# A chunk's second part ahead of the next unit's first part, in the state-space layer of a two-layer decoder step

## The chip, the cores and the metric

One core of a Trainium2 chip runs the whole kernel as one program. The metric is device time in microseconds (us), the median of the timed runs. Engines are named as the profile names them: PE (matmuls), PEld (its weight loads), DVE, ACT and POOL (elementwise work), SP (issues most of the DMAs). Each works through its own queue in program order.

## The reference, cut to what matters

Two groups of tokens, 512 of a prompt and 8x4 of a sample group, pass through one state-space layer (Mamba-2, chunked) and one windowed attention layer with shared keys and values. Everything here concerns the first layer. Its core, for 32 heads in 4 groups and chunks of 128 tokens:

```
cb = einsum("bctgn,bcsgn->bcgts", Cc, Bc)
m = einsum("bcgts,bgjcts->bcgjts", cb, seg)          # seg = exp of decay differences, lower triangle
y_diag = einsum("bcgjts,bcsgjp->bctgjp", m, X)
chunk_states = einsum("bctgn,bgjct,bctgjp->cbgjpn", Bc, decay_in, X)
s_final, s_in = scan(step, s0, (chunk_decay, chunk_states))   # s = decay * s + chunk_state
y_off = einsum("bctgn,cbgjpn,bgjct->bctgjp", Cc, s_in, exp(a_cs))
y = y_diag + y_off
```

Before it stands an input projection (1024 to 5152 columns, a convolution of width 4 and a silu on part of them), behind it a gate, a norm and an output projection.

## The kernel before, in words

**Filler and units.** The input projection is the filler: a generator that yields after every matmul. One projected tile of 128 columns is 24 matmuls into `pa` (256 tokens) and 24 into `pb` (288 tokens): 8 slices of the contraction, three passes each with a high and a low half of the weights (`whi`, `wlo`). For every tile ACT makes `whi` (L205) and DVE `wlo` (L206) from a loaded `wraw`. A conv tile is then copied out by ACT (L343, L348, L349), multiplied once by ACT (L639 `co`) and three times by DVE (L641 `co`); ACT takes a tanh (L643) and DVE writes the result (L644, L645). A z tile takes a tanh on ACT (L680 `zth`) and one DVE operation (L681 `uz`).

The state-space work is cut into units, per group g: chunk 0, chunk 1, quad 0, chunk 2, chunk 3, quad 1. A chunk is 128 prompt tokens of the group's 8 heads, a quad four sample rows. A unit is a generator too. The loop at L915 starts unit u, runs half a pace of filler matmuls (`PACE` is 57, 62, 64 and 44 for the four groups), lets unit u-1 go on to its next part, runs the other half, and lets unit u-1 go on once more.

**A chunk's first part** loads `m` (L728, 512 KB: decay sums, the same for all partitions) and, for c > 0, `ea` (L754); ACT makes decays of it in place with eight Relu (L730) and one Exp (L732); PE makes `cbp` (two products, L734 and L735) and `xp` (four transposes); ACT copies `btok` (L740); DVE makes `xdt`, `xdd`, `cbm` and the masked `m` (L746 to L749).

**A chunk's second part** is on PE `csp` (L757, the chunk's state), for c > 0 `yo` (L765), and `yd` (L774, eight products that read `m` and `xdt`). They are taken out by DVE: `st` (L762, into which POOL has put the decayed old state, L761), `ea` (L767), `v` (L778); in chunk 0 by ACT (L769, L776). It is all the chunk has left: the loop's second call of a chunk finds nothing.

**A quad's first part** loads four states `s` (L804) and makes `cbp`, `xp` and `yos` (L818) on PE; its second part makes `yds`, `yot` and three products `up` (L859), its third a fourth `up`. DVE adds each `up` to a state (L862), and ACT's queue sends the state out (L863).

**Buffers.** All products of the units share one pool of five PSUM tiles (`pss`, L163); `pa` and `pb` have another of three (`pj`, L160). `m` has two buffers, `xdt` and `xdd` together three (L742, L743), `ea` one, the quads' `s` five.

**What sets the order.** PE's order in this layer is that of the code (`pinned`, L139: matmuls are held in program order). The order on DVE, ACT, POOL and SP is set by a scheduler that works from its own model of the times, so it can change with any edit, and no engine leaves its order when the kernel runs.

Of the kernel before, what the change touches and what calls it, by code (L numbers as in the profile page):

```python
# [127 lines left out]
def tile_yoco_step(  # L128
# [569 lines left out]
    def skip_one():  # L698
        if not skips:
            return  # L700
        g, i = skips.pop(0)
        vi = v_t[g][:, i, :]
        nc.vector.scalar_tensor_tensor(vi, xs_t[g][:, i, :], dsk[:, 4 * g + i:4 * g + i + 1], vi, op0=ALU.mult, op1=ALU.add)
        v_done.add((g, i))
        if i < z_done.get(g, 0):
            gate_mul_a(g, i)
# [192 lines left out]
    def run(n):  # L899
        for _ in range(n):  # L900
            if next(fill, 0) == 0:
                return

    units = [(f, (g, i)) for g in range(4) for f, i in
             ((ssm_chunk, 0), (ssm_chunk, 1), (ssm_quad, 0), (ssm_chunk, 2), (ssm_chunk, 3), (ssm_quad, 1))]
# [8 lines left out]
    live = []  # L914
    for u in range(len(units) + 1):  # L915
        pace = PACE[min(u, len(units) - 1) // 6]
        if u < len(units):
            live.append(units[u][0](*units[u][1]))
            next(live[u])
        skip_one()  # L920
        run(pace // 2)
        if u:
            next(live[u - 1], 0)
            skip_one()
            run(pace - pace // 2)
            next(live[u - 1], 0)
            if u == len(units):
                run(10000)
            if u % 6 == 0:
                skips += [(u // 6 - 1, i) for i in range(4)]  # L930
            skip_one()
        else:
            run(pace - pace // 2)
# [702 lines left out]
    def run(n):  # L1636
        m = min(n, ahead[0]) if n > OCN else 0
        ahead[0] -= m
        for _ in range(n - m):
            if next(fill, 0) == 0:  # L1640
                return

    units = [(f, (h, i)) for h in range(ATH - 1) for f, i in
             ((attend, 0), (sample, 0), (attend, 1), (attend, 2), (sample, 1), (attend, 3))]
# [6 lines left out]
    live = []  # L1651
# [113 lines left out]
```

## Time and profile before

| what | value |
|---|---|
| median of 3 runs | 926.12 us (924.83 to 927.18) |
| the profiled execution | 932.11 us; span on the core 930.2 us |
| state-space stage (units on PE) | about 76 to 345 us of the span |
| PE busy, whole span | 908.9 us, 98% |
| DVE, ACT, POOL busy | 687.5, 489.9 and 163.0 us |
| mean granted TensorE clock | 0.996 |

The stages follow each other: input projection and state-space units (to 345 us), output projection, keys and values, attention. A long PE wait shows as idle time before an instruction, with the name of what released it.

### The profile page before, as it was taken

The page shows a single profiled execution, that of the slowest core. Times are in us where ns is not written, and L with a number is a line of the kernel's source. Part 1 is how long each engine was busy: PE and PEld are TensorE (multiplying, and loading weights), DVE is VectorE, ACT ScalarE, POOL GpSimd, SP SyncE. Part 2 cuts the span into 40 slices and gives each one's busy share as a digit, 9 for nine tenths or more (in the row PEclk, how much of TensorE's full clock was granted, in tenths as well). Part 3 has the DMA queues.
Part 4 walks back from the last instruction along what each step waited for, and adds up shares of the span by engine and source line. Part 5 has one row for each costly group of instructions (what it writes and reads, how often), then busy time and mean ns, then how long its engine had stood idle before and what let it go on. Part 6 is the DMA issues. An engine that isn't in the chain of part 4 may idle for free.

```text
span 930.2 us, 21888 instructions
## 1 busy us (share of the span) xinstructions
PE 908.9 (98%) x8671; PEld 847.9 (91%) x8671; DVE 687.5 (74%) x1435; ACT 489.9 (53%) x1140; POOL 163.0 (18%) x212
## 2 busy tenths in 40 slices
PE   8999999999999999999999999999999999999997
PEld 7989888888989889999999999999899999989997
DVE  6998899989799899644489335876677766778732
ACT  6678655655566655422255213555455555557642
POOL 2031344433514642111101001000000000000021
PEclk9999999999999999999999999999999999999999
DMA  8224365355364442536277556757768868774511
GB/s 295 93 74 155 104 206 166 121 170 170 134 201 161 149 165 101 156 108 228 90 256 227 183 184 196 265 182 264 252 203 262 280 204 267 270 256 155 194 49 49
DMA packets 80573, 168.48 MB, mean 181 GB/s; under 512 B 19990, under 2 KB 37736, under 8 KB 79960
## 3 DMA queue, kind: packets, MB, share of 16 engines
q1 hardware_dynamic: 73784, 154.60, 50.5%
q10 hardware_dynamic: 5616, 9.75, 2.8%
q0 software_dynamic: 1072, 2.74, 1.1%
q8 instruction: 68, 1.11, 0.5%
q14 instruction: 33, 0.27, 0.1%
HBM read 141.14 MB, written 25.93 MB: 180 GB/s over the span
## 4 chain that ended last, share of the span: by engine, by line
PE 82%; DVE 9%; DMA 4%; ACT 2%; issue 2%; POOL 0%; SPq 0%; POOLq 0%; DVEq 0%; ACTq 0%
PE pa L146 33%; PE pb L146 28%; PE sp L146 3%; PE pv L146 2%; PE so L146 2%; PE s L146 2%; DVE wlo L206 2%; DMA kc<-ck 1%; PE yd L146 1%; DMA m<-aed 1%; DVE co L641 1%; PE csp L146 1%; PE w L149 1%; PE ptp L149 1%; PE xp L149 1%
## 5 line engine op out<-in xcount | busy, mean ns | idle before, releaser
L205 ACT ACTIVATE whi<-wraw 128x1024 fp32r<-128x1024 f32 x69 | 72.8, 1056 | 97.0 <-PE pb L146 57.2
L206 DVE TENSOR_TENSOR wlo<-wraw,whi 128x1024 fp32r<-128x1024 f32 x69 | 89.6, 1298 | 45.1 <-ACT whi L205 44.7
L146 PE MATMUL pa<-bq,whi 128*128 128x272 f32 x512 | 103.1, 296 | 0.0
L146 PE MATMUL pb<-nl,whi 128*128 128x288 f32 x280 | 84.0, 300 | 0.0
L146 PE MATMUL pb<-nh,wlo 128*128 128x288 f32 x280 | 83.5, 298 | 0.0
L146 PE MATMUL pb<-nh,whi 128*128 128x288 f32 x280 | 83.4, 298 | 0.0
L146 PEld LDWEIGHTS pa<-bq,whi 128*128 128x128 f32 x512 | 81.2, 189 | 0.9
L146 PE MATMUL pa<-nh,whi 128*128 128x256 f32 x280 | 81.1, 290 | 0.5 <-DVE uz L681 0.5
L146 PE MATMUL pa<-nl,whi 128*128 128x256 f32 x280 | 80.7, 288 | 0.0
L146 PE MATMUL pa<-nh,wlo 128*128 128x256 f32 x280 | 80.1, 286 | 0.0
L146 PE MATMUL pb<-bq,whi 128*128 128x272 f32 x384 | 77.2, 296 | 1.3 <-DVE kv L1230 1.1
L146 PE MATMUL pa<-bq,wlo 128*128 128x272 f32 x256 | 74.2, 290 | 0.0
L641 DVE SCALAR_TENSOR_TENSOR co<-cb,cvp,co 128x568 f32<-128x568 f32 x72 | 64.0, 892 | 1.5 <-ACT co L639 0.9
L146 PEld LDWEIGHTS pb<-bq,whi 128*128 128x128 f32 x384 | 60.8, 189 | 2.6 <-DVE kv L1230 1.3
L1289 ACT ACTIVATE whi<-wraw 128x512 fp32r<-128x512 f32 x64 | 40.1, 627 | 35.2 <-PE pb L146 16.8
L146 PEld LDWEIGHTS pb<-nl,whi 128*128 128x128 f32 x280 | 53.0, 189 | 4.4 <-issue 4.4
L146 PEld LDWEIGHTS pa<-nh,whi 128*128 128x128 f32 x280 | 53.8, 192 | 2.6 <-issue 1.9
L146 PE MATMUL pb<-bq,wlo 128*128 128x272 f32 x192 | 55.5, 289 | 0.0
L146 PEld LDWEIGHTS pa<-nl,whi 128*128 128x128 f32 x280 | 53.8, 192 | 1.4 <-issue 1.4
L146 PEld LDWEIGHTS pb<-nh,wlo 128*128 128x128 f32 x280 | 53.1, 190 | 2.2 <-issue 2.2
L146 PEld LDWEIGHTS pa<-nh,wlo 128*128 128x128 f32 x280 | 53.8, 192 | 0.9 <-issue 0.9
L146 PEld LDWEIGHTS pb<-nh,whi 128*128 128x128 f32 x280 | 53.0, 189 | 0.8 <-issue 0.8
(408 smaller groups left out, 2788.0 us busy)
## 6 DMA issues: line engine op xcount, KB each, us to landing
wraw<-w_in SPq DMA_DIRECT2D x40, 512.0 KB
kc<-ck SPq DMA_DIRECT2D x32, 640.0 KB
vc<-cv SPq DMA_DIRECT2D x32, 640.0 KB
wraw<-wb SPq DMA_DIRECT2D x32, 512.0 KB
s<-s SPq DMA_DIRECT2D x32, 256.0 KB
m<-aed SPq DMA_DIRECT2D x16, 512.0 KB
ssmS<-s ACTq DMA_DIRECT2D x32, 256.0 KB
wraw<-w_out SPq DMA_DIRECT2D x16, 512.0 KB
```

The source lines that it names most:

```text
L146: pin(nc.tensor.matmul(*a, **k))
L149: pin(nc.tensor.transpose(*a))
L205: a = nc.scalar.activation(hi, raw, AF.Copy)
L206: b = lo_eng.tensor_tensor(lo, raw, f32(hi), op=ALU.subtract)
L641: nc.vector.scalar_tensor_tensor(o, cb[:, k:k + n], cvp[:, ti, k:k + 1], o, op0=ALU.mult, op1=ALU.add)
L1289: nc.scalar.activation(hi, src[p][j], AF.Copy)
```

## The change

Where unit u-1 is a chunk, its second part now stands directly ahead of unit u's first part, and the two calls half a pace and a whole pace later are left out. Quads go as before. No instruction is added or taken away.

```diff
     for u in range(len(units) + 1):
         pace = PACE[min(u, len(units) - 1) // 6]
+
+        joined = u and units[u - 1][0] is ssm_chunk
+        if joined:
+            next(live[u - 1], 0)
         if u < len(units):
             live.append(units[u][0](*units[u][1]))
             next(live[u])
         skip_one()
         run(pace // 2)
         if u:
-            next(live[u - 1], 0)
+            if not joined:
+                next(live[u - 1], 0)
             skip_one()
             run(pace - pace // 2)
-            next(live[u - 1], 0)
+            if not joined:
+                next(live[u - 1], 0)
```

Below, chunk c of group g is written g.c. Three places show how the rows move.

On PE, where chunk 0.1 ends and quad 0 of group 0 begins (filler rows left out between the rows shown: 28 in the kernel before). Before:

```order
L149 MATMUL cbp<-ident,bp 128x128
L146 MATMUL cbp<-CT,bp 128x16
L149 MATMUL xp<-ident,xpd 128x128 x4
L146 MATMUL yos<-s_1279,cp 32x512
L146 MATMUL yos<-s_1281,cp 32x512
L146 MATMUL yos<-s_1283,cp 32x512
L146 MATMUL yos<-s_1285,cp 32x512
```

and, 28 filler rows later:

```order
L146 MATMUL csp<-xdd,btok 128x512
L146 MATMUL yo<-CT,st 128x128 x4
L146 MATMUL yd<-m,xdt 64x128 x8
```

Now:

```order
L146 MATMUL csp<-xdd,btok 128x512
L146 MATMUL yo<-CT,st 128x128 x4
L146 MATMUL yd<-m,xdt 64x128 x8
L149 MATMUL cbp<-ident,bp 128x128
L146 MATMUL cbp<-CT,bp 128x16
L149 MATMUL xp<-ident,xpd 128x128 x4
L146 MATMUL yos<-s_1300,cp 32x512
```

The chunk's three PSUM tiles and the quad's three are now asked for in one run of rows: six out of a pool of five. The same holds at both quads of each group.

On DVE, the rows up to the removal of `csp` of chunk 1.1 (`st`). Before:

```order
L681 SCALAR_TENSOR_TENSOR uz<-zth,pa 128x256
L829 TENSOR_TENSOR xdt<-xp,tok 128x512
L644 SCALAR_TENSOR_TENSOR CT<-cb,co 128x512
L645 SCALAR_TENSOR_TENSOR CT<-cb,co 128x32
L220 SCALAR_TENSOR_TENSOR btr<-cbp,csts,btr 128x128
L823 TENSOR_TENSOR cbs<-cbp,csts 128x16
L839 TENSOR_TENSOR ms<-ms,cbs 128x128
L206 TENSOR_TENSOR wlo<-wraw,whi 128x1024
L681 SCALAR_TENSOR_TENSOR uz<-zth,pb 128x288
L832 TENSOR_TENSOR xdd<-xp,tok 128x512
L762 TENSOR_TENSOR st<-csp,st 128x512
```

Now:

```order
L644 SCALAR_TENSOR_TENSOR BT<-cb,co 128x512
L645 SCALAR_TENSOR_TENSOR BT<-cb,co 128x32
L641 SCALAR_TENSOR_TENSOR co<-cb,cvp,co 128x568
L681 SCALAR_TENSOR_TENSOR uz<-zth,pa 128x256
L641 SCALAR_TENSOR_TENSOR co<-cb,cvp,co 128x568
L762 TENSOR_TENSOR st<-csp,st 128x512
L767 TENSOR_TENSOR ea<-yo,ea 128x512
```

`st` has moved up past the quad's rows and one `wlo`; ahead of it stand still the `co` and `uz` rows of filler tiles.

On ACT, the rows ahead of the second quad of group 0, with the evacuation of the filler tile that PE ends there (L348 to L639) and the Relu and Exp of chunk 1.0 (`m`). Before:

```order
L643 ACTIVATE cb<-co 128x568
L205 ACTIVATE whi<-wraw 128x1024
L348 COPY cb<-pb 128x256
L349 COPY cb<-pb 128x8x4
L219 ACTIVATE btr<-cbp,csts 128x128
L635 COPY cvo<-cb 128x27
L639 ACTIVATE co<-cb,cvp 128x568
L825 COPY yos<-yos 128x512
L730 ACTIVATE m<-m,tok 128x128 x6
```

Now:

```order
L730 ACTIVATE m<-m,tok 128x128 x6
L732 ACTIVATE m<-m 128x1024
L205 ACTIVATE whi<-wraw 128x1024
L348 COPY cb<-pb 128x256
L349 COPY cb<-pb 128x8x4
L643 ACTIVATE cb<-co 128x568
L635 COPY cvo<-cb 128x27
L639 ACTIVATE co<-cb,cvp 128x568
L219 ACTIVATE btr<-cbp,csts 128x128
L825 COPY yos<-yos 128x512
```

The Relu and Exp rows have gone from behind the tile's evacuation to ahead of it. With them the load of that `m` has moved in SP's queue: before it stood behind four loads of quad states and a `wraw`, now it stands behind two of the four.

## Prediction

> **What bounds the kernel now.** I read the page's busy times first, then the table by stretches over the state-space stage, with groups 1 and 2 and a short stretch of 2 us, then PE's waits from 60 to 345 us (in all, times, longest).
>
> ```profile
> PE 908.9 (98%) x8671; PEld 847.9 (91%) x8671; DVE 687.5 (74%) x1435; ACT 489.9 (53%) x1140; POOL 163.0 (18%) x212
> ```
> ```profile
> core 0: us, PE busy (x) PEld busy (x) DVE busy (x) ACT busy (x) POOL busy (x), PEclk, DMA share, GB/s
> 140.00:211.00 71.00, 69.32 (x573) 61.78 (x572) 66.82 (x94) 42.80 (x109) 28.50 (x31) 1.00 0.46 153
> 211.00:290.00 79.00, 75.44 (x592) 67.49 (x591) 68.36 (x105) 45.92 (x116) 28.97 (x31) 0.96 0.51 166
> 216.00:218.00 2.00, 2.00 (x12) 2.00 (x11) 2.00 (x4) 1.97 (x6) 0.00 (x0) 0.50 0.29 88
> ```
> ```profile
> PE xp L149 <- DVE xs L644: 2.1, 1, 2.1
> PE up L146 <- DVE cbm L748: 1.4, 1, 1.4
> PE yd L146 <- ACT yos L825: 1.2, 1, 1.2
> PE pa L146 <- DVE uz L681: 0.5, 1, 0.5
> ```
>
> PE bounds the stage, and DVE stands close behind: 66.82 of 71 us in group 1. The waits list says that PE loses 5.2 us. The short stretch shows what a wait costs besides: just behind the 2.1 us wait the granted clock is 0.50. The first rows behind that wait and behind the 1.4 us wait (at 214.63 and 258.83), picked out of the chain of waits, each below the same work undisturbed:
>
> ```profile
> 70.11 2.85 PE pa L146 x24
> 214.63 4.20 PE pa L146 x24
> 239.08 2.32 PE pb L146 x16
> 258.83 3.12 PE pb L146 x16
> ```
>
> The same matmuls took 4.20 instead of 2.85 us after the first wait, 1.35 us more, and after the second the first sixteen alone took 0.8 us more. I take 1.35 for both, 2.7 together. (Group 1, with the waits of 1.2 and 0.5 us, kept a granted clock of 1.00.) So all that a better order could win here is 5.2 + 2.7 = 7.9 us, 0.85% of the kernel.
>
> **The change, part by part.** PE has the same matmuls before and after. What changes is when the others must have delivered.
>
> *Inputs of the second part.* `csp`, `yo` and `yd` come half a pace (28 to 32 filler matmuls, about 0.12 us each by the x24 row, so some 3.5 us) sooner behind the first part. Of the 16 chunks 0.0 had the least time between its masked `m` and `yd`:
>
> ```profile
> 81.43 1.22 DVE L749 TENSOR_TENSOR m<-m,cbm 128x1024 f32<-128x1024 f32 x1
> ```
>
> `m` was done at 82.65 and `yd` ran at 89.95 (row below), 7.3 us later. Cost 0; the cover that is left is some 3.8 us, and where DVE falls that much further behind, `yd` itself waits (-0, +3 at one place). Something is freed too: `xdd` of odd chunks had to wait for the previous chunk's `csp` to give up one of three buffers, and now does not. I give this no price of its own; it shows in the places of the rows below.
>
> *Fewer changes between filler and units.* One return to filler is saved per chunk. The rows from the chain:
>
> ```profile
> 85.06 0.44 PE xp L149 x4
> 85.50 1.07 PE pa L146 x9
> ...
> 89.95 1.02 PE yd L146 x16
> 90.97 0.86 PE pb L146 x5
> ```
>
> Behind `xp` a filler matmul takes 0.12 us, as always; the five behind `yd` take 0.17 instead of 0.13, 0.2 us together. Over 16 chunks the gain is 0 to 3.2 us; I take the middle, -1.6, since no row shows `yd` followed by `cbp`.
>
> *PSUM, the new wait.* Where a quad follows a chunk (twice per group), six tiles in a row are asked of five buffers, so the quad's `yos` must wait until DVE has taken out `csp` (`st`, L762). Behind `yos` the filler is queued, so all of PE stands. The time that PE gives to DVE is what lies between:
>
> ```profile
> 100.25 0.86 PE csp L146 x2
> 101.11 0.89 PE yo L146 x8
> 102.00 1.02 PE yd L146 x16
> ```
>
> ```profile
> 161.48 0.27 PE L149 MATMUL cbp<-ident,bp 128*128 128x128 f32 x1
> 162.30 1.06 PE L146 MATMUL yos<-s,cp 128*32 128x512 f32 x8
> ...
> 167.17 1.02 PE L146 MATMUL csp<-xdd,btok 128*128 128x512 f32 x2
> ```
> ```profile
> 168.65 0.41 DVE L681 SCALAR_TENSOR_TENSOR uz<-zth,pa 128x256 f32<-128x256 f32 x1
> ...
> 175.83 0.68 DVE L762 TENSOR_TENSOR st<-csp,st 128x512 f32<-128x512 f32 x1
> ```
>
> `yo` and `yd` take 0.89 + 1.02, the quad's `cbp` and `xp` 0.82 (161.48 to 162.30): 2.7 us from the end of `csp` to `yos`, 3.6 from its start. Before, `st` ended 8.3 us behind `csp` at 1.1 (168.19 to 176.51), and no matmul stood waiting for it. What stands ahead of `st` now, at each place (`csp` now begins where the quad's `cbp` stood):
>
> - 0.1: two `co` of a tile whose evacuation was long done. No stall.
> - 0.3: ACT has the Relu and Exp of chunk 1.0 ahead of the tile's evacuation, and that needs its `m`. Rows of ACT and SP:
>
> ```profile
> 118.20 5.36 SPq L804 DMA_DIRECT2D s<-s  x4
> 124.13 0.38 SPq L728 DMA_DIRECT2D m<-aed  x1
> ```
> ```profile
> 128.86 1.04 ACT L205 ACTIVATE whi<-wraw 128x1024 fp32r<-128x1024 f32 x1
> 130.51 0.87 ACT L639 ACTIVATE co<-cb,cvp 128x568 f32<-128x568 f32 x1
> 131.74 1.87 ACT L730 ACTIVATE m<-m,tok 128x128 f32<-128x128 f32 x6
> 134.55 1.06 ACT L732 ACTIVATE m<-m 128x1024 f32<-128x1024 f32 x1
> ```
> ```profile
> 195.97 7.81 DMA m<-aed
> 250.54 4.32 DMA m<-aed
> ```
>
>  The load goes out behind two of the four `s` loads, at about 120.9, and takes 4.3 to 7.8 us: 125.2 at best. Then eight Relu (8/6 x 1.87 = 2.5), Exp 1.06, `whi` 1.04, three copies and a tanh (some 1.4) and `co` 0.87: 132.1; DVE's `co` and `st`, some 0.75 each, with what lies between: 134. PE is at `yos` at 131.5 (the quad's `cbp` stood at 127.9). Stall 0.5 (landing early, rows overlapping) to 5; I take 2.7.
> - 1.1: DVE is the late one. `st` now stands directly behind the `uz` of 168.65 and a `co`, so it ends at 169.7 at the earliest, if DVE, which is full here, has the same work ahead; PE wants `yos` at 161.5 + 3.6 = 165.1. That is 4.6 us; if the stall at 0.3 has already let DVE catch up, 0.5. I take 2.6.
> - 1.3 and 2.1: the first Relu rows of the next chunk but one (2.0, 2.2) have moved ahead of the evacuation on ACT, where they wait for `m`.
>
> ```profile
> ACT m L730 <- DMA m<-aed: 12.9, 8, 3.6
> ```
> ```profile
> 189.12 6.29 SPq L804 DMA_DIRECT2D s<-s  x3
> 195.97 0.38 SPq L728 DMA_DIRECT2D m<-aed  x1
> ```
>
>  For 1.3 the load goes out behind two of the three `s`, at 193.3, lands at 197.6 to 201.1, and the same string on ACT and DVE (some 6.5 us) ends `st` at 204 to 207.6; PE is at `yos` at 202.2. Stall 0 to 5.6, I take 3.0. For 2.1, reckoned in the same way, 0 to 3: 1.6.
> - 2.3, 3.1, 3.3: the rows ahead of `st` are of tiles done a half before, or z tiles with one short DVE operation. 0.3 in all.
>
> Together 10.2 us of new stalls (bounds 1 and 19). A stall of 1.4 us or more has cost 1.35 us more at the low clock: three of four such, 4.1. Behind a stall PE comes later to everything, so DVE, which was the late one at the four old waits, is in time there: the old 5.2 and 2.7 us go.
>
> The Trainium skill, "TensorE: Matmul & The Clock Gate", section "Why this matters for your kernels", says that only idle gaps over about 3 us between bursts bring the clock down. By it neither old nor new stalls would cost clock, and the sum would be 10.2 - 5.2 - 1.6 = 3.4 us. The row at 216 us, behind a gap of 2.1 us, says otherwise, and the trace decides.
>
> *SP and POOL.* Loads of `m` go out up to 5 us sooner, since `yd` of the chunk two back is done sooner; the distance from that `yd` to the use is what it was. POOL's `st` product (L761) needs the previous chunk's state, a whole pace away as before. Cost 0 each; bounds -1 and +1 by a landing that shifts a neighbour.
>
> **The sum.** New stalls 10.2, clock 4.1, old waits -5.2, old clock loss -2.7, changes saved -1.6: +4.8 us. The profiled execution took 932.11 us, so 936.9; it ran 0.65% above the median of 926.12, so I put the difference on the median: 930.9.
>
> **The rivals.**
>
> *The waits only change their place.* In group 1 DVE has 66.82 us of work in 71; PE must wait for it somewhere, now or later. If the stalls at 0.3 and 1.1 let DVE catch up, 1.3 and 2.1 do not stall: 5.6 us of stalls, 2.7 of clock, -9.5 of old: -1.2, 925. For it speaks the full DVE; against it that at 1.3 and 2.1 a DMA is late, which PE's coming later does not help, since the loads move with it. Chance 0.22 for within 0.3%, the least that a measurement here can tell from no change (2.8 us).
>
> *Faster.* `st` is in time everywhere: then nothing is lost, and 7.9 + 1.6 = 9.5 us can go, of which I would expect two thirds: -6.3, 920. This decides where `st` ends within 2.7 us of `csp`. For it: `st` now stands higher in DVE's queue, and `xdd` needs no free buffer. Against: DVE needed 8.3 us at 1.1. Chance 0.20.
>
> *Much slower.* ACT stands on its first Relu until `m` lands, and each of the four stalls is near its upper bound: 18 us, clock 5.4, -9.5 of old: +14, 940. For it: 7.81 us for one load. Chance 0.13; the forecast itself has 0.45.
>
> So slower 0.58, same 0.22, faster 0.20. The range leaves out about one in ten on each side: 919 to 940; the forecast's own is 928 to 936.
>
> **What would show it.** In the profile after: a wait of PE `yos` on DVE `st`, two to four times, 1 to 5 us, at the quads that follow 0.3, 1.1, 1.3 and 2.1; low granted clock behind them; the four old waits gone or smaller; the ACT waits on `m` not below 12.9 us. If PE shows no `yos` wait, the forecast is wrong in its main term; if the old waits are still there beside the new, it is too low.

## The result, and the profile after

The changed kernel took 948.74 us in the median of five runs (945.91 to 951.50), the kernel before 927.18 in the same comparison (924.83 to 927.85): a ratio of 1.0241, 95% interval 1.0215 to 1.0267, or 21.6 us. The forecast was slower, 930.9 in a range of 919 to 940: the sign and the place were right, the size was not.

The profiled execution of after took 948.74 us, its median; that of before, 932.11, lay 5 us above its own. In spans they differ by 16.7 us (946.9 and 930.2). Outside the state-space stage before took 1.7 us longer than after (641.8 us in after, 643.5 in before), with late loads as the visible part (PE waited 2.2 us for the first weights at 6 us and 1.4 for `kc`, against 0.5 and nothing), so inside the stage the difference is larger, 18.4 us.

The whole stage in one row each, from its first `cbp` to the first matmul of the projection behind it (columns as in the tables of the prediction: the stretch, its length, busy us of PE, PEld, DVE, ACT and POOL, granted clock, DMA share, GB/s). Before:

```profile
76.70:363.42 286.72, 281.46 (x2293) 251.19 (x2291) 257.88 (x386) 173.74 (x418) 111.31 (x116) 0.99 0.47 155
```

After:

```profile
76.39:381.52 305.13, 285.66 (x2292) 252.90 (x2291) 260.18 (x386) 173.21 (x418) 111.21 (x116) 0.97 0.45 145
```

PE stands 19.5 instead of 5.3 us (length less busy time), and its work takes 4.2 us more at a lower clock. DVE's work is nearly the same, 260 and 258 us, but DVE stands 45 us instead of 29. PE's waits in the stage of after:

```profile
PE yos L146 <- DVE st L762: 17.1, 5, 5.2
PE xp L149 <- DVE xs L644: 2.1, 2, 1.8
PE pa L146 <- DVE uz L681: 0.3, 1, 0.3
```

The wait that the prediction named is there and is nearly all of it: the quad's `yos` on `st`, five times, at 131.3 (behind chunk 0.3, 2.1 us), 168.6 (1.1, 4.5), 210.3 (1.3, 3.0), 251.6 (2.1, 2.4) and 290.1 (2.3, 5.2). The last is the one that the prediction had dismissed. SP, ACT, DVE and PE there, each in order of time:

```profile
280.47 0.42 SPq L728 DMA_DIRECT2D m<-aed  x1
```
```profile
288.62 0.40 ACT L730 ACTIVATE m<-m,tok 128x128 f32<-128x128 f32 x1 [8.89 <-DMA m<-aed]
288.93 1.04 ACT L205 ACTIVATE whi<-wraw 128x1024 fp32r<-128x1024 f32 x1
...
291.19 0.86 ACT L639 ACTIVATE co<-cb,cvp 128x568 f32<-128x568 f32 x1
```
```profile
290.01 1.23 DVE L206 TENSOR_TENSOR wlo<-wraw,whi 128x1024 fp32r<-128x1024 f32 x1 [5.12 <-ACT whi L205]
...
292.08 2.50 DVE L641 SCALAR_TENSOR_TENSOR co<-cb,cvp,co 128x568 f32<-128x568 f32 x3
294.50 0.68 DVE L762 TENSOR_TENSOR st<-csp,st 128x512 f32<-128x512 f32 x1
```
```profile
286.25 1.02 PE L146 MATMUL csp<-xdd,btok 128*128 128x512 f32 x2
...
295.24 1.08 PE L146 MATMUL yos<-s,cp 128*32 128x512 f32 x4 [5.19 <-DVE st L762]
```

Read them from the top. The load of chunk 3.0's `m` goes out at 280.5 and takes 8.1 us. ACT has its first Relu at the head of its queue and stands 8.89 us for it. Behind the Relu stands a weight's high part (`whi`), which does not read `m` at all; DVE's low part (`wlo`) waits for that, 5.12 us; behind it are a conv output and three taps, and only then `st`. `csp` had been done since 287.1, where `yo` begins; `st` takes it out at 294.5, 7.4 us later. The matmuls that stand between take up 2.9 of these; the rest PE waits.

### The profile page after: what moved, and what is told of

The parts are those of the page before. It is cut to its first block, busy times and chain, and to the rows that moved or that the text cites. A ratio compares the mean times of both kernels' runs of the same rounds, so it can differ in the third digit from the quotient of the medians.

```text
span 946.9 us, 21901 instructions
## 1 busy us (share of the span) xinstructions
PE 914.0 (97%) x8671; PEld 851.1 (90%) x8671; DVE 690.0 (73%) x1435; ACT 489.9 (52%) x1140; POOL 162.9 (17%) x212
## 4 chain that ended last, share of the span: by engine, by line
PE 81%; DVE 8%; DMA 4%; ACT 4%; issue 2%; SPq 0%; POOL 0%; POOLq 0%; DVEq 0%; ACTq 0%
PE pa L146 33%; PE pb L146 27%; DMA m<-aed 3%; PE sp L146 3%; PE pv L146 2%; PE so L146 2%; PE s L146 2%; DVE wlo L206 1%; DVE co L641 1%; PE yos L146 1%; PE w L149 1%; PE ptp L149 1%; PE yd L146 1%; PE csp L146 1%; DVE v L703 1%
## 5 line engine op out<-in xcount | busy, mean ns | idle before, releaser
L641 DVE SCALAR_TENSOR_TENSOR co<-cb,cvp,co 128x568 f32<-128x568 f32 x72 | 62.1, 864 | 1.9 <-ACT co L639 0.9
L730 ACT ACTIVATE m<-m,tok 128x128 f32<-128x128 f32 x128 | 42.1, 393 | 24.7 <-DMA m<-aed 24.7
```

What stands on the lines that cost most here:

```text
L641: nc.vector.scalar_tensor_tensor(o, cb[:, k:k + n], cvp[:, ti, k:k + 1], o, op0=ALU.mult, op1=ALU.add)
L730: nc.scalar.activation(m_t[:, h, :], m_t[:, h, :], AF.Relu, scale=-1.0, bias=tok[:, c, 0, 8 * g + h:8 * g + h + 1])
```

## The experiments

All stand against the kernel before in runs of the same comparison, where its median was 927.1 to 927.6. Theories: **R**, the loss is the run of six tiles in five buffers (the ring); **T**, the second part is due half a pace sooner from engines without slack, and the ring is only the first place where that shows; **L** or **O**, the loads of `m` and the Relu rows on ACT; **2**, R and L side by side; **S** and **Q**, DVE's slack or the order of the queues; **P**, POOL's adds (later). Each edit also lets the scheduler choose a new order on DVE, ACT, POOL and SP, so a difference of a microsecond or two need not come from what the edit is meant to change.

| kernel | median, us | ratio to before, 95% interval |
|---|---|---|
| changed | 948.74 | 1.0241 (1.0215 to 1.0267) |
| `join_cc` | 940.65 | 1.0130 (1.0109 to 1.0151) |
| `join_cq` | 934.04 | 1.0070 (1.0053 to 1.0087) |
| `after_yos24` | 947.97 | 1.0214 (1.0194 to 1.0234) |
| `eighth` | 941.11 | 1.0150 (1.0125 to 1.0176) |
| `quarter` | 930.76 | 1.0042 (1.0028 to 1.0056) |
| `late34` | 923.88 | 0.9963 (0.9950 to 0.9976) |
| `late78` | 926.38 | 0.9979 (0.9967 to 0.9991) |
| `after_mhold` | 941.07 | 1.0159 (1.0137 to 1.0181) |
| `before_nom` / `after_nom` | 927.23 / 936.65 | 1.0001 (0.9990 to 1.0013) / 1.0096 (1.0077 to 1.0115) |
| `yos24_nom` | 934.15 | 1.0062 (1.0042 to 1.0082) |
| `before_tap` / `after_tap` | 923.47 / 935.53 | 0.9957 (0.9942 to 0.9972) / 1.0098 (1.0074 to 1.0123) |
| `before_nom_tap` / `after_nom_tap` | 924.70 / 928.69 | 0.9977 (0.9960 to 0.9993) / 1.0022 (1.0009 to 1.0034) |
| `before_nossq` / `after_nossq` | 922.05 / 941.37 | 0.9946 (0.9928 to 0.9963) / 1.0150 (1.0133 to 1.0168) |
| `after_nom_tap_nossq` | 921.82 | 0.9941 (0.9926 to 0.9956) |

### Half of the change each, and a yos that comes later

`join_cc`, `join_cq`: which joins are kept.

```
-        joined = u and units[u - 1][0] is ssm_chunk
+        joined = u and u < len(units) and units[u - 1][0] is ssm_chunk and units[u][0] is ssm_chunk
```

(`join_cq` with `is not ssm_chunk` at the end.)

> Only the joins from chunk to chunk are kept; where a quad follows, the chunk's second part stands half a pace later, as before. Theory R (ring: the loss is the quad's yos, sixth of six tiles in five PSUM buffers, which waits for DVE's st): no yos wait on st, the old waits somewhere between 0 and 5 us; 920 to 928, same as before or a little faster. Theory T (time: the second part comes half a pace too early for a full DVE and ACT wherever it is joined; the ring is only the first place where that shows): about half of the loss stays, 935 to 940, as waits of csp, yd or xp.

> Only the joins from chunk to quad are kept. Theory R: all of the loss is here, yos waits on st of 14 to 20 us in all, 943 to 952. Theory T: about half of it, 935 to 940.

`after_yos24`: a `yield` ahead of the quad's `yos`, and 24 filler matmuls there.

```
+        late = 24 * (u < len(units) and units[u][0] is ssm_quad)
+        run(late)
+        if late:
+            next(live[u])
-        run(pace // 2)
+        run(pace // 2 - late)
```

> The changed kernel, but the quad's yos matmuls come 24 filler matmuls (2.9 us) behind its xp, so DVE has 5.6 instead of 2.7 us from the end of csp. Theory R: each yos wait is 2.9 us shorter: 2.1, 4.5, 3.0, 2.4, 5.2 become 0, 1.6, 0.1, 0, 2.3, 4 us in all, and most of the low clock goes: 928 to 935. Theory T: DVE and ACT deliver no sooner, so other matmuls wait in its place (yot, up, xp, yd); the sum of PE's waits in the stage stays at 12 us or more, 940 or more.

R fell in all three. PE's longest waits in the stage, of `join_cc`, of `join_cq` and of `after_yos24`:

```profile
PE xp L149 <- DVE xs L644: 6.6, 2, 3.4
PE yd L146 <- ACT yos L825: 1.4, 2, 1.0
```
```profile
PE yos L146 <- DVE st L762: 4.8, 2, 3.8
PE xp L149 <- DVE xs L644: 3.9, 2, 2.5
```
```profile
PE xp L149 <- DVE xs L644: 12.3, 2, 6.3
PE yos L146 <- DVE st L762: 3.2, 4, 1.5
PE up L146 <- DVE cbm L748: 1.8, 1, 1.8
```

`join_cc` has no `yos` wait on `st` and still costs 13 us. In `after_yos24` the `yos` waits shrink as reckoned, from 17.1 to 3.2 us, and nothing is won: PE now stands 12.3 us for `xs` at the start of groups 2 and 3. The buffer ring says where PE waits, not how long. That is T's picture, though T's numbers for the two halves (equal parts) were off too. ACT's wait for `m` went to different sides: 31.8 us in `join_cc` and 5.7 in `join_cq`, against 12.9 before; that this makes the halves unequal was not tested.

### Where the second part stands

`eighth`, `quarter`, `late34`, `late78`: the chunk's second part at 1/8, 1/4, 3/4 and 7/8 of the pace behind the following unit's first part (the changed kernel is 0, the kernel before 1/2), here `quarter`:

```
-        run(pace // 2)
+        run(pace // 4)
+        if u and units[u - 1][0] is ssm_chunk:
+            next(live[u - 1], 0)
+        run(pace // 2 - pace // 4)
```

> The kernel before with a chunk's second part an eighth of a pace (5 to 8 filler matmuls, about 0.8 us) behind the following unit's first part. No yos waits on st, since csp comes behind yos. Theory 2: the run of six tiles now ends with yd, which needs only the quad's cbp to be taken out, so that part goes; the loads of m are drawn forward nearly as far as in the changed kernel, so 932 to 940. Theory T: between the quarter (930.8) and none (948.7), near 940.

> The kernel before with a chunk's second part a quarter of a pace behind the following unit's first part (half a pace in the kernel before, directly ahead in the changed one). The run of six tiles is gone. Theory T: cost in proportion to the time taken away, 934 to 940. Theory O: m is given up a quarter sooner, so also a cost, but jumpy: 927 to 940. If only the run of six tiles mattered: 924 to 928.

> The kernel before with a chunk's second part three quarters of a pace behind the following unit's first part. Theory T: more time for DVE, so 918 to 925. Theory O: m is given up later still, loads and Relu rows stand later; ACT's wait for m below 12.9 us, 920 to 927, unless m's own product then comes late and yd of the chunk after next waits.

> The kernel before with a chunk's second part seven eighths of a pace behind the following unit's first part. At three quarters PE's waits in the stage were down to 0.9 us, so there is little left to win: 921 to 926. If the state or m's buffer now comes late (m is given up an eighth later still), waits of yd or csp: 925 to 930.

In order of the place: 948.7, 941.1, 930.8, 927.1, 923.9, 926.4. The later the second part, the better, up to three quarters; the steep part is the first quarter, which gives back 18.0 of the 21.6 us. `quarter` came out better than T had said (934 to 940) and inside O's range (927 to 940); the cost is not in proportion to the time taken away. For `eighth` theory 2 said 932 to 940 and T near 940, and the time hardly tells them apart. The waits do:

```profile
PE xp L149 <- DVE xs L644: 5.4, 2, 3.2
PE yd L146 <- DVE cbs L823: 4.5, 2, 3.5
ACT m L730 <- DMA m<-aed: 9.4, 6, 3.2
```

ACT stands less for `m` than in the kernel before (12.9 us), so the loads do not explain these 13.5 us; and `yd`, the sixth tile here, now waits until the quad's `cbp` has been taken out (`cbs`), which theory 2 had held to be free. PE waits for DVE in another place, as T has it. The stage of `late34`:

```profile
78.10:357.70 279.60, 277.55 (x2293) 248.01 (x2291) 255.10 (x386) 173.96 (x419) 114.06 (x116) 1.00 0.48 158
PE pa L146 <- DVE uz L681: 1.2, 1, 1.2
PE yos L146 <- ACT st L769: 0.9, 1, 0.9
```

Two waits are all that is left, 2.1 us, the first of them at the stage's very end, and the clock is 1.00. `late34` beats both kernels; it is 0.4% faster than before. At 7/8 (926.4 us, just above the 921 to 926 expected) the wait of this kind has grown again. By the medians that place is too late, but the two intervals overlap:

```profile
PE yos L146 <- ACT st L769: 2.3, 2, 1.2
```

### The loads of m

`after_nom`, `before_nom`: no loads of `m`; the Relu reads a constant tile.

```
-        dma(m_t, dap(aed, (32 * c + 8 * g) * 128, [[0, 128], [128, 8], [1, 128]]))
-            nc.scalar.activation(m_t[:, h, :], m_t[:, h, :], AF.Relu, scale=-1.0,
+            nc.scalar.activation(m_t[:, h, :], tri, AF.Relu, scale=-1.0,
```

> The changed kernel without the 16 loads of m (512 KB each): the Relu reads a constant tile instead, so ACT never stands on a load there; instructions on PE, DVE and ACT are the same in number. Theory L (load: ACT's Relu waits for m, behind it the weight's high part and DVE's low part, behind that st): the yos waits at 0.3, 1.3, 2.1 and 2.3, 12.7 us in all, fall below 1 us each, only 1.1 may keep up to 4.5; 925 to 934. If st is late by DVE's own amount of work and its order (theory D): yos waits of 12 us or more stay, 942 or more.

> The kernel before without the 16 loads of m (the Relu reads a constant tile). It is the partner of the changed kernel without loads, 936.7. Theory O: the cost of the change comes through the loads, so the two should lie within 3 us of each other: 933 to 938 here. Theory T: the change costs without loads too; this one stays at 920 to 928, and the difference to 936.7 is 9 us or more.

Before does not miss the loads (1.0001), as T said; O had put the two kernels within 3 us of each other. After is 12.1 us faster without them, but 9.4 us remain, so L is a part and not the whole, and its own number (925 to 934) was missed. The `yos` waits at 0.3, 1.3 and 2.3 are gone, as L said; 4.6 us at 1.1 remain, and 2.0 at 2.1, where L had put less than 1.

`after_mhold`: one DVE operation of a single element reads `m` behind `v`, so that `m`'s buffer is given up later.

```
+ nc.vector.tensor_tensor(hold[0:1, 0:1], m_t[0:1, 0, 0:1], v[0:1, 0, c * 128:c * 128 + 1], op=ALU.add)
```

> The changed kernel with one more DVE operation of a single element per chunk, which reads m and v behind v: m's buffer is given up some 3 to 6 us later, so the load of m for the chunk after next and its Relu rows stand later on SP and ACT, behind the high part of a weight that was behind them. PE's order is that of the changed kernel. Theory O (order: m given up sooner draws loads and Relu rows forward in queues that work in order, ACT stands on the load, and behind it whi, wlo and the conv chain): ACT's wait for m falls from 24.7 to 13 us or less and DVE's wait for whi from 25.7 to 18 or less; 928 to 938. Theory T (time: outputs of the second part are due half a pace sooner from a DVE with no slack): 943 to 951, the waits only change their place.

It won 7.7 of 21.6 us, between the two theories. DVE's wait for `whi` fell as O had said; the expected fall of ACT's own wait did not come. ACT's wait for `m` in before, after and `after_mhold`, and then DVE's wait for `whi` in the same three:

```profile
ACT m L730 <- DMA m<-aed: 12.9, 8, 3.6
```
```profile
ACT m L730 <- DMA m<-aed: 24.7, 8, 8.9
```
```profile
ACT m L730 <- DMA m<-aed: 24.2, 11, 4.4
```
```profile
DVE wlo L206 <- ACT whi L205: 19.2, 14, 3.1
```
```profile
DVE wlo L206 <- ACT whi L205: 25.7, 11, 5.1
```
```profile
DVE wlo L206 <- ACT whi L205: 6.8, 8, 1.6
```

So it is not the sum of ACT's standing that costs, but what is queued behind it while it stands. At 1.3 and 2.3 the Relu rows now come behind `whi` and the tile's evacuation (at 2.3 `co` runs at 279.2 and the first Relu at 282.3), and the `yos` waits of 3.0 and 5.2 us there are gone. At 0.3 the first Relu still stands ahead of `whi`, and 1.0 us of wait is left.

`yos24_nom` takes away both, the loads and the short time that DVE has until `yos`.

> The changed kernel without the loads of m and with the quad's yos 24 filler matmuls later: both suspected causes are taken away at once. Theory 2 (two causes: loads and Relu rows drawn forward, 12 us; the run of six tiles where DVE is behind, 9.5 us): 925 to 930, PE's waits in the stage below 5 us. Theory T (DVE has half a pace less, and every way of waiting for it costs the same): the yos waits turn into waits of xp, up or pa, 934 to 938.

934.2 us lies in T's range, not in theory 2's. Without loads and with `yos` 2.9 us later PE still waits 4.2 us for `xs`, 1.6 for `st` and 1.5 for `uz`.

### DVE's slack

One of the three convolution taps on DVE (L641) is left out in four kernels: change or not, loads or not. From 76.7 to 363.4 us the taps that stay kept DVE busy for 30.7 instead of 49.8 us in the kernel before and 32.0 instead of 47.9 in the changed one, 16 to 19 us less.

```
-        for k in range(1, 4):
+        for k in range(1, 3):
```

> The kernel before with two instead of three taps of the convolution on DVE (one is left out): 18 operations of 0.92 us, 16.6 us, less for DVE in the stage. PE's waits in the stage of before, 5.2 us with 3 us of low clock, should shrink to 0 to 2 us: 919 to 925.

> The changed kernel with one tap of the convolution left out, so DVE has 16.6 us of slack in the stage. Theory S (no slack: the half pace taken from DVE can't be given by a full engine): with slack the difference to its partner before falls from 21.6 to 5 us or less, 920 to 930. Theory Q (queue order: ACT stands on a load of m and DVE behind it, whatever DVE has to do): the 12 us that hang on the loads stay, 932 to 940.

> The kernel before without loads of m and with one tap left out: the floor for the stage, 918 to 925.

> The changed kernel without loads of m and with one tap left out. Theory S: no more than 3 us over its partner before, no yos wait over 1 us; 919 to 927. If the 9.5 us that the change costs without loads came from order alone (each queue in its new order, whatever the slack), 6 us or more of it stay: 927 to 933.

The cost of the change (after less before, of the medians):

| | with loads of `m` | without |
|---|---|---|
| three taps | 21.6 | 9.4 |
| two taps | 12.1 | 4.0 |

Both matter, and neither alone is the cause. Slack takes away about half in each column; the part that hangs on the loads stays at 8 to 12 us in each row, so Q holds for it. `after_tap` came where Q put it; `after_nom_tap` lies, by its cost of 4.0 us, between the two (its time, 928.7, in the range for order alone). What was left there was in the main one place, 1.1:

```profile
PE yos L146 <- DVE st L762: 5.7, 2, 4.6
```

### What is late at 1.1

The wait at the quad behind 1.1 was much the same in the changed kernel, `after_mhold`, `after_nom`, `after_tap` and `after_nom_tap` (4.5 to 4.8 us), with loads or without, with three taps or two. DVE and POOL of the changed kernel there:

```profile
159.83 0.68 DVE L746 TENSOR_TENSOR xdt<-xp,tok 128x512 f32<-128x512 f32 x1
...
162.67 2.40 DVE L749 TENSOR_TENSOR m<-m,cbm 128x1024 f32<-128x1024 f32 x1
164.98 1.88 DVE L641 SCALAR_TENSOR_TENSOR co<-cb,cvp,co 128x568 f32<-128x568 f32 x1
166.79 2.37 DVE L206 TENSOR_TENSOR wlo<-wraw,whi 128x1024 fp32r<-128x1024 f32 x1
169.08 0.80 DVE L641 SCALAR_TENSOR_TENSOR co<-cb,cvp,co 128x568 f32<-128x568 f32 x1
...
172.27 0.68 DVE L762 TENSOR_TENSOR st<-csp,st 128x512 f32<-128x512 f32 x1
```
```profile
159.29 1.52 POOL L761 TENSOR_TENSOR st<-st,dec 128x512 f32<-128x512 f32 x1
160.78 1.36 POOL L711 TENSOR_TENSOR v<-v,uz 128x544 f32<-128x544 f32 x1
162.10 5.97 POOL L716 TENSOR_TENSOR ssq<-ssq,uz 128x544 f32<-128x544 f32 x3
```

While POOL adds the squares of group 0's gate (L716), DVE's rows take twice their time: `m` 2.40 instead of 1.21 us, a tap 1.88 instead of 0.80, `wlo` 2.37 instead of 1.21. `before_nossq`, `after_nossq`, `after_nom_tap_nossq` leave these adds out:

```
-        nc.gpsimd.tensor_tensor(ssq, ssq, uz, op=ALU.add)
```

> The kernel before with POOL's adds of the squares (ssq, L716, 15 in all) left out; DVE's order stays. DVE rows that stood beside them (m at 156.59: 2.36 instead of 1.22 us) take their usual time. Theory P (POOL's long adds slow DVE beside them, and that is the lateness at 1.1): the old waits at 169 and 175, 1.7 us, go: 923 to 927. Without it: 926 to 929.

> The changed kernel with POOL's adds of the squares left out. Theory P: the four DVE rows between 161.2 and 169.1, which took 8.2 us, take 4.6; the yos wait at 1.1 falls from 4.46 to below 1.5 us, the one at 2.1 by 1 us; 940 to 945. Without it: 946 to 951, and 4 us or more of wait at 1.1.

> The changed kernel without loads of m, with one tap left out and without POOL's adds of the squares. With loads and taps gone, all that was left of PE's waits was yos, 4.64 at 1.1 and 1.06 at 2.1, and 4.0 us against its partner (928.7 to 924.7). Theory P: both waits below 1 us and 923 to 926, nothing of the change's cost is left. Without it: the 4.6 us stay, 927 to 930.

P holds for the place. In `after_nossq` the same DVE rows take their usual time:

```profile
164.47 1.21 DVE L749 TENSOR_TENSOR m<-m,cbm 128x1024 f32<-128x1024 f32 x1
165.60 0.80 DVE L641 SCALAR_TENSOR_TENSOR co<-cb,cvp,co 128x568 f32<-128x568 f32 x1
166.32 1.21 DVE L206 TENSOR_TENSOR wlo<-wraw,whi 128x1024 fp32r<-128x1024 f32 x1
```

The wait at 1.1 fell from 4.5 to 1.0 us and the kernel to 941.4. The wait at 2.1, which should have lost 1 us, did not (2.4 and 2.7). Without loads it was 2.0, with a tap less besides 1.1, and with the adds gone too it was not seen: no single one of the three takes it away. Before gained 5.0 us as well, a little more than expected, so the adds are a tax on both kernels and explain only some 2.3 us of the difference (21.6 less 19.3). With loads, one tap and adds gone, the changed kernel stands at 921.8, under `before_nom_tap` (924.7, which still has the adds), and one `yos` wait of 1.7 us remains, at 1.1, not below 1 as expected. What of the change's cost is left there is not measured, since a kernel before without all three was not run. If the adds cost it the same 5.0 us as above, it would stand near 919.7, and some 2 us would be left; that is an estimate.

## Why the prediction was wrong in size

The table has the prediction's own terms in us, and beside them what the two profiled executions show. The low clock is summed over stretches of 1 us, busy time of PE times what its clock lacked of 1.00. The changes saved are what is left over of PE's busy time (4.2 us more in after, 5.1 of them by the clock), and so were not measured by themselves.

| term | forecast | measured |
|---|---|---|
| `yos` at 0.3 | 2.7 | 2.1 |
| at 1.1 | 2.6 | 4.5 |
| at 1.3 | 3.0 | 3.0 |
| at 2.1 | 1.6 | 2.4 |
| at 2.3, 3.1, 3.3 and 0.1 | 0.3 | 5.2, at 2.3 |
| low clock, new | 4.1 | 8.5 |
| old waits | -5.2 | -2.9 |
| old low clock | -2.7 | -3.4 |
| changes saved | -1.6 | -0.9 |
| sum, in the stage | 4.8 | 18.4 |

- **Place and mechanism: right.** The wait that was named, on the tile that was named, at the four places that were named. At 0.3 the working (load, eight Relu, Exp, `whi`, conv, `st`) came as written and was 0.6 us off. At 1.3 the 3.0 us are partly luck: the load took 7.7 us, the upper end of its range, only one Relu and no Exp stood ahead of `whi`, and PE itself came later to `yos`. Its signs came, too: such waits (five instead of two to four), low clock behind some, ACT's wait for `m` at 24.7 us, above the 12.9 of before. So did its sign of being too low: the `xp` wait on `xs` was still there beside the new ones, 2.1 us in both kernels.
- **The step that failed first: "2.3 ... 0.3 in all".** The wait there was 5.2 us, the largest single miss of the sum. The step looked at the rows that DVE has directly ahead of `st` and took their tiles for long done. It did not follow them to ACT: at 2.3, as at 1.3, the `whi` ahead of them was queued behind the first Relu of the next group's chunk, whose load was 8.1 us on its way. The rule that had been applied at 1.3 was not applied at 2.3; with 1.3's own bounds, 0 to 5.6, it would have held.
- **1.1: the middle instead of the end.** The row gave 4.6 if DVE has the same work ahead; the rival "it has caught up by then" was mixed in at half weight. DVE could not catch up, since POOL's adds were slowing it; without them the wait was 1.0 us. The adds had rows in the trace of before too; there `m` of 1.1 took 2.36 us, and 1.21 without them.
- **"Behind a stall DVE is in time there: the old 5.2 and 2.7 us go."** Wrong by nearly half for the waits: PE still waited 2.1 us for `xs`, the wait that also stood first in `join_cc` and `after_yos24`. A stall of PE does not let DVE catch up when DVE itself stands on ACT through it: DVE's wait for `whi` rose from 19.2 to 25.7 us.
- **The clock: 8.5 instead of 4.1.** Four waits cost clock, three had been counted: the two long ones cost double, 6.8 us at half clock instead of 3.4, two of the `yos` waits (3.0 and 2.4 us) cost none, and one of `xp` (1.85 us) did. The last section has the rows.
- **"SP and POOL ... Cost 0 each."** Right for what was counted, the issue and the state's product; wrong in that the earlier loads drew the Relu rows forward on ACT. The prediction had those rows in its 0.3, 1.3 and 2.1, but not as one cause; without the loads the changed kernel was 12.1 us faster.
- **The rivals.** "Much slower" had 18 us of stalls where 17.1 came, but by luck: its four places gave 12.0 of them, the rest came at 2.3. It still ended at 940: its clock loss was 5.4 where 8.5 came, and it took away 9.5 us of old waits, old clock and savings where 7.2 went.
- The median moved by 21.6 us, the stage of the profiled executions by 18.4. The 3.2 us between them are not traced to a place.

## What to carry to other kernels

Giving a buffer up sooner is no gain by itself: here the scheduler pulled the next load and its first reader forward in queues that work in order, and what stood behind that reader then waited for the DMA. When PE and a second engine are both near full, price a move by the lead that it takes from the second engine and not by the first wait that becomes visible; loosening that wait (24 matmuls more ahead of `yos`) moved it and won next to nothing. Try the opposite direction too: here the second part a quarter of a pace later was the faster kernel.

## What the runs showed of the hardware that was not expected

**The clock falls on a grid.** These rows show the granted clock (the last column but two) in and behind four gaps of PE in after. Of the gap at 1.1, which ended at 173.01, only the low stretch is shown, which began inside it.

```profile
131.32:133.40 2.08, 0.00 (x1) 0.00 (x0) 2.08 (x5) 0.73 (x2) 1.77 (x5) 1.00 0.50 114
133.48:136.88 3.40, 3.40 (x15) 1.74 (x16) 3.40 (x5) 1.21 (x2) 1.51 (x2) 0.50 0.83 309
171.02:177.84 6.82, 4.83 (x21) 3.17 (x22) 6.79 (x14) 4.53 (x11) 4.68 (x9) 0.50 0.41 156
210.29:213.24 2.95, 0.00 (x0) 0.00 (x0) 2.88 (x5) 2.95 (x9) 1.63 (x4) 1.00 0.90 342
213.24:217.00 3.76, 3.76 (x29) 2.92 (x30) 3.65 (x6) 2.81 (x6) 2.63 (x3) 1.00 0.36 124
223.06:224.91 1.85, 0.00 (x1) 0.01 (x1) 1.11 (x3) 1.46 (x2) 0.00 (x0) 1.00 0.38 153
225.64:229.04 3.40, 3.40 (x18) 3.40 (x17) 3.40 (x6) 0.00 (x0) 0.00 (x0) 0.50 0.13 22
```

A gap of 1.85 us cost 3.4 us at half clock; one of 2.95 us cost nothing. All low stretches, in this and the other runs, are 3.4, 6.8 or 10.2 us long, save the one that each execution ends in, and in after they begin at 133.48, 171.02, 225.64 and 293.90: 11.0, 16.0 and 20.0 times 3.41 us apart. So a gap's length alone does not set its price, and the prediction's rule "1.4 us or more costs 1.35" did not hold. That its place on the grid of 3.41 us decides fits the rows, but what idle share of a step it takes, these runs don't settle: a gap of 1.42 us cost clock in before, gaps of 1.37 and 1.77 us in `quarter` did not. The Trainium skill, "TensorE: Matmul & The Clock Gate", section "What's actually happening", states a free-running window of 3413 ns, with which the grid agrees; the same page's rule of gaps over about 3 us (section "Why this matters for your kernels"), which the prediction set against the trace, does not fit the 1.85 us.

**POOL slows some of DVE's rows and not others.** In the rows at 1.1, `m`, the taps and `wlo`, whose operands all lie in SBUF, took twice their time beside POOL's add; `xdt` at 159.83, which reads `xp` from PSUM, took its usual 0.68 us beside POOL's product at 159.29. The Trainium skill, "SBUF — State Buffer", section "SBUF: two separate sides", says that a DVE operation with two SBUF inputs and a POOL operation that reads SBUF shut each other out of a shared port for a whole instruction. The rows agree as to which operations are slowed, and `after_nossq` shows that the slowing goes with POOL's adds; that one waits for a whole instruction of the other can't be read from them.
